# Weight sums of a seven-product gate: from VectorE additions to accumulating transfers

## The chip, the cores and the metric

The kernel runs on one core of a Trainium2 chip. The metric is the device time of one execution in microseconds; the median of several executions is compared. TensorE multiplies, VectorE (DVE) and ScalarE (ACT) work elementwise, GpSimd (POOL) and SyncE (SP) are used here only to issue transfers.

## The reference

The program is a stack of four layers on a 512 x 1024 input in fp32: two layers of a first kind (spatial gating, a state-space mixer, differential attention, three gates, a feed-forward part), then two of a second kind. The change touches the gates of the first kind. Of each such layer, cut to what matters:

```python
proj = h @ w_in[layer]                       # h: 512 x 1024
g = sigmoid(gates).reshape(b, s, 3, 1024)    # gates: the last 3072 columns of proj
merged = (g[:, :, 0] * (y_a @ w_branch_a[layer])
          + g[:, :, 1] * (y_b @ w_branch_b[layer])
          + g[:, :, 2] * (y_c @ w_branch_c[layer]))
x = x + merged @ w_out[layer]
```

## The kernel before, in words

Every fp32 matmul is made of three: a weight tile `wr` that a transfer has brought is split by ScalarE into a rounded part `wh` (a cast) and by VectorE into the rest `wl = wr - wh`; the activations are split in the same way, and `mm3` (L512) adds high x high, high x low and low x high in PSUM. A weight tile holds 2 x 128 rows and 512 columns, 512 KB. There are four `wr` buffers and three each of `wh` and `wl`. PSUM has four `pm` banks and four `px` banks.

**Order of the work.** No engine call runs directly. The class `Order` records each one (`record`, L185) with a cost, a priority and its dependences; `schedule` (L240) lays all of them out in time by that model, and `issue` (L380) emits them in this order and pins the order on each engine's queue. A call made inside `hurry` or with a `bonus` gets a priority far ahead of its place. A transfer is modelled as its bytes over 360 per ns on one shared line (L204), plus 740 ns after SyncE's issue and 2240 ns after GpSimd's (`LANDED`, L132). `after=op` makes a call wait for `op` in this model.

**The gates.** `layer1` (L1062) makes the first gate with plain matmuls and the other two (columns of `w_in`, 1024 wide) with `tm7` (L583), a scheme of Strassen's kind: the 1024 x 1024 weights are cut into quarters b11, b12, b21, b22 of 512 x 512, and seven products of a half of the tokens with a quarter or a sum of quarters, instead of eight, give the gate. The combinations of the activations are made once in `combos` (L555). A product is 24 matmuls of 512 columns into two banks and needs two `wr` tiles ("halves", of 256 rows). Before, each quarter is loaded once. VectorE makes the sums: `q` = b11 + b12 in four heap slots of 512 columns, later `q` += b22, then `q` += b21 (four operations each), and b12 += b22 in place (two operations of 1024 columns). The products run in the order b11, q, q, b12, b22, b21, q; the first `q` product goes into `px`. Their results are combined in the gate's tiles `sg` and go through a tanh (`fin`). This runs in four stages: third and second gate of each layer of the first kind. Between them lie the products of `branch`.

**The parameters.** `load_params1` (L805) brings the packs `pn`, `pa` and `pb` at a layer's start, for the first layer on SyncE's queue, for the second on GpSimd's. `pa` has 3180 columns, 1590 KB. At once it derives `nlam`, `nega`, `slg2` and `wt` from `lam`, `alog`, `slg` and `ws` in it. In the first layer the constants `cst` (592 KB) follow on SyncE's queue; `norm` (L692) needs the ones in them.

## Time and profile before

| | us |
|---|---|
| median of 3 runs | 2515.24 (2515.04 to 2518.61) |
| the profiled execution | 2517.48 |
| its span, first to last instruction | 2515.6 |
| TensorE busy | 2496.1 |
| VectorE busy | 1742.5 |
| ScalarE busy | 1215.3 |
| GpSimd busy | 52.7 |
| transfers of SyncE's queue | 241.03 MB |
| transfers of GpSimd's queue | 20.33 MB |

The span is that of one profiled execution; the time of the same execution is 1.9 us longer. "Busy" of TensorE counts overlapping matmuls once, so it does not tell at what pace they follow each other; the pace is read from a stretch of the chain and the number of matmuls in it. Nearly all instructions carry one line (L385, where `issue` emits them), so the rows are told apart by the names of the tiles: out<-in. The chain is the work that ended last, followed back from the last instruction.

### The profile page before, as it was taken

What the parts mean: (1) busy time and instruction counts of PE and PEld (TensorE: products, weight loads), DVE (VectorE), ACT (ScalarE), POOL (GpSimd) and SP (SyncE); (2) the same over time, 40 slices, a digit from 0 to 9 for tenths busy, and PEclk for the clock granted to TensorE, in tenths of its full rate; (3) what the DMA queues carried; (4) which work ended last, traced back from release to release, by engine and by line L of the source; (5) the groups of instructions that cost most, each with busy time, mean ns of one, the idle gap of its engine ahead of it and who ended that gap; (6) DMA issues with size and microseconds to landing.
All of it is one profiled execution on the core that took longest, in us unless ns stands there. A gap on an engine that the chain in (4) does not pass through costs nothing.

```text
span 2515.6 us, 33045 instructions
## 1 busy us (share of the span) xinstructions
PE 2496.1 (99%) x12158; PEld 2111.6 (84%) x12158; DVE 1742.5 (69%) x3497; ACT 1215.3 (48%) x2210; POOL 52.7 (2%) x103
## 2 busy tenths in 40 slices
PE   8999999999999999999999999999999999999999
PEld 7888888888888888898888888888898888988887
DVE  7679878657566346598878486663369987679783
ACT  5494734434444234757544254442247564356552
POOL 0000000000000000101000000000000000000000
PEclk9999999999999999999999999999999999999999
DMA  7444343343333444434343343333433123432222
GB/s 219 100 120 105 70 110 101 109 150 102 100 95 116 133 111 78 152 66 101 85 107 102 101 143 101 96 97 117 137 109 97 54 68 95 142 105 68 68 76 84
DMA packets 160642, 263.48 MB, mean 105 GB/s; under 512 B 11504, under 2 KB 71296, under 8 KB 160224
## 3 DMA queue, kind: packets, MB, share of 16 engines
q1 hardware_dynamic: 152864, 241.03, 34.0%
q0 software_dynamic: 7616, 20.33, 2.9%
q8 instruction: 96, 1.57, 0.3%
q14 instruction: 66, 0.54, 0.1%
HBM read 241.33 MB, written 14.75 MB: 102 GB/s over the span
## 4 chain that ended last, share of the span: by engine, by line
PE 88%; DVE 7%; DMA 2%; ACT 1%; issue 1%; SPq 0%; DVEq 0%; ACTq 0%
PE pm L385 68%; PE px L385 20%; DVE wl L385 2%; DMA wr<-in_w_in_dram 2%; DVE sg L385 1%; DMA pa<-in_pa_dram 1%; ACT p L385 1%; DVE q L385 0%; DVE p L385 0%; DVE sptl L385 0%; DMA cst<-in_cst_dram 0%; ACT wh L385 0%; DVE so L385 0%; SPq L385 0%; DVE gs L385 0%
## 5 line engine op out<-in xcount | busy, mean ns | idle before, releaser
L385 DVE TENSOR_TENSOR wl<-wr,wh 128x1024 fp32r<-128x1024 f32 (+3 forms) x413 | 488.9, 1185 | 598.9 <-ACT wh L385 593.9
L385 ACT CAST wh<-wr 128x1024 fp32r<-128x1024 f32 (+3 forms) x413 | 421.6, 1022 | 828.3 <-PE pm L385 658.3
L385 PE MATMUL pm<-wh,hh 128*128 128x512 f32 (+2 forms) x608 | 229.5, 377 | 0.0
L385 PE MATMUL pm<-wl,hh 128*128 128x512 f32 (+2 forms) x608 | 227.3, 374 | 0.0
L385 PE MATMUL pm<-wh,hl 128*128 128x512 f32 (+2 forms) x608 | 225.8, 374 | 0.0
L385 PE MATMUL pm<-hh,wh 128*128 128x512 f32 x512 | 199.8, 390 | 0.0
L385 PE MATMUL pm<-hh,wl 128*128 128x512 f32 x512 | 199.5, 390 | 0.0
L385 PE MATMUL pm<-hl,wh 128*128 128x512 f32 x512 | 199.2, 389 | 0.0
L385 PE MATMUL pm<-gl,wh 128*128 128x512 f32 x384 | 154.1, 401 | 0.0
L385 PE MATMUL pm<-gh,wh 128*128 128x512 f32 x384 | 153.3, 399 | 0.0
L385 PE MATMUL pm<-gh,wl 128*128 128x512 f32 x384 | 152.5, 397 | 0.0
L385 PE MATMUL pm<-wh,gh 128*128 128x512 f32 (+2 forms) x384 | 143.6, 375 | 0.9 <-ACT wh L385 0.9
L385 PE MATMUL pm<-wl,gh 128*128 128x512 f32 (+2 forms) x384 | 143.4, 374 | 0.0
L385 PE MATMUL pm<-wh,gl 128*128 128x512 f32 (+2 forms) x384 | 142.6, 372 | 0.0
L385 PE MATMUL pm<-acth,wh 128*128 128x512 f32 x352 | 136.9, 389 | 0.0
L385 PE MATMUL pm<-actl,wh 128*128 128x512 f32 x352 | 136.9, 389 | 0.0
L385 PE MATMUL pm<-acth,wl 128*128 128x512 f32 x352 | 136.9, 389 | 0.0
L385 PEld LDWEIGHTS pm<-wh,hh 128*128 128x128 f32 x608 | 114.3, 188 | 15.7 <-issue 3.3
L385 PEld LDWEIGHTS pm<-wl,hh 128*128 128x128 f32 x608 | 114.4, 188 | 14.3 <-issue 1.9
L385 PEld LDWEIGHTS pm<-wh,hl 128*128 128x128 f32 x608 | 114.3, 188 | 13.8 <-issue 1.4
L385 PE MATMUL px<-hl,wh 128*128 128x512 f32 x320 | 124.5, 389 | 0.0
L385 PE MATMUL px<-hh,wl 128*128 128x512 f32 x320 | 124.5, 389 | 0.0
(479 smaller groups left out, 5669.1 us busy)
## 6 DMA issues: line engine op xcount, KB each, us to landing
wr<-in_w_in_dram SPq DMA_DIRECT2D x151, 512.0 KB, 3.8
wr<-in_ffn_w_up_dram SPq DMA_DIRECT2D x176, 256.0 KB, 3.1
wr<-in_ffn_w_down_dram SPq DMA_DIRECT2D x44, 512.0 KB, 3.5
wr<-in_w_out_dram SPq DMA_DIRECT2D x40, 512.0 KB, 3.6
wr<-in_w_in_dram SPq DMA_DIRECT2D x40, 384.0 KB, 3.5
xr<-xd SPq DMA_DIRECT2D x48, 256.0 KB, 4.9
xd<-xr SPq DMA_DIRECT2D x40, 256.0 KB, 3.2
m<-ad POOLq DMA_DIRECT2D x32, 256.0 KB, 7.3
```

Of the source, the lines that this page charges most:

```text
L385: ins = f(*args, **kw).ins
```

## The change

`tm7` no longer adds quarters on VectorE. `q` and `b2` are now pairs of `wr` tiles: SyncE loads a quarter into them, and transfers on GpSimd's queue with `accum_op=ALU.add` add another quarter from HBM to what lies there. b11 is loaded twice, b22 fetched three times (once plainly), b21 and b12 as the sums need them. The order of products is b11, b21, q = b11 + b12, b2 = b12 + b22, q += b22, b22, q += b21, and all go into `pm`. Loading with four `wr` buffers becomes loading with five (NWR, also in `wload`). To a layer's `pa` pack the columns of `ws`, `lam`, `slg` and `alog` (912 of 3180) no longer belong; two packs `pl` (400 columns) and `pw` (512) bring them on GpSimd's queue into heap slots, after the first matmuls of the layer (`late_params1`, called in `layer1`), and what was derived from them is derived there. The planner's model counts an accumulating transfer at half the rate.

```diff
--- before.py
+++ after.py
@@ -24,6 +24,7 @@
 KD = D // P
 EPS = 1e-6
 NSLOT = 68
+NWR = 5
 NPM = 4
 
 GM = 512
@@ -79,10 +80,10 @@
     "pn": [("ang", "attn_norm_g", columns, 8)],
     "pa": [("cw", "ssm_conv_w", columns, 48), ("cb", "ssm_conv_b", columns, 12),
            ("bs", "gm_b_s", rows, 512), ("vg", "gm_v_norm_g", rows, 512), ("dtb", "ssm_dt_bias", rows, 16),
-           ("alog", "ssm_a_log", rows, 16), ("dsk", "ssm_d", rows, 16), ("sng", "ssm_norm_g", rows, 1024),
-           ("qg", "da_q_norm_g", rows, 64), ("kg", "da_k_norm_g", rows, 64), ("slg", "da_subln_g", rows, 128),
-           ("lam", "da_lambda", rows, 256),
-           ("ws", "gm_w_s", lambda v: v.transpose(2, 0, 1).reshape(P, -1), 512)],
+           ("dsk", "ssm_d", rows, 16), ("sng", "ssm_norm_g", rows, 1024),
+           ("qg", "da_q_norm_g", rows, 64), ("kg", "da_k_norm_g", rows, 64)],
+    "pw": [("ws", "gm_w_s", lambda v: v.transpose(2, 0, 1).reshape(P, -1), 512)],
+    "pl": [("lam", "da_lambda", rows, 256), ("slg", "da_subln_g", rows, 128), ("alog", "ssm_a_log", rows, 16)],
     "pb": [("fng", "ffn_norm_g", columns, 8), ("fcw", "ffn_conv_w", columns, 132), ("fcb", "ffn_conv_b", columns, 44)],
     "pc": [("ng", "norm_g_2", columns, 8), ("qag", "mla_q_a_norm_2", columns, 2), ("kvg", "mla_kv_a_norm_2", columns, 1),
            ("cw2", "conv_w_2", lambda v: v.reshape(3, 4, P).transpose(2, 0, 1).reshape(P, -1), 12),
@@ -201,7 +202,7 @@
             n = 4.0
             for d in outs[0].shape:
                 n *= d
-            op.dma = n / 360.0
+            op.dma = n / (180.0 if "accum_op" in kw else 360.0)
         op.succ, op.bufs = [], set()
         deps = {after: 0} if after is not None else {}
         for ap, wr in [(a, False) for a in ins] + [(a, True) for a in outs]:
@@ -442,10 +443,11 @@
     def pmix(self):
         return self.tile(self.px, [P, T], F32, "px", "px", 8 - NPM)
 
-    def pack(self, key, l, eng=None):
+    def pack(self, key, l, eng=None, temp=False, op=None):
         items = PACK[key]
-        t = self.param(key, sum(i[3] for i in items))
-        (eng or self.nc.gpsimd).dma_start(out=t, in_=self.a[key][l])
+        n = sum(i[3] for i in items)
+        t = self.slot(key, [P, n]) if temp else self.param(key, n)
+        (eng or self.nc.gpsimd).dma_start(out=t, in_=self.a[key][l], after=op)
         q, o = {}, 0
         for nm, _, _, n in items:
             q[nm] = t[:, o:o + n]
@@ -491,7 +493,7 @@
         nc = self.nc
         n = sum(c[1] for c in cols)
         keep, nc.bonus = nc.bonus, bonus
-        wr = self.tile(self.wp, [P, nk, n], F32, "wr", "wr", 4)
+        wr = self.tile(self.wp, [P, nk, n], F32, "wr", "wr", NWR)
         off = 0
         for c0, cn in cols:
             nc.sync.dma_start(out=wr[:, :, off:off + cn],
@@ -582,8 +584,11 @@
 
     def tm7(self, w, c0, parts, c, fin):
 
+
         nc = self.nc
         v = nc.vector
+        rows = lambda kh, u: slice((kh * 4 + u * 2) * P, (kh * 4 + u * 2 + 2) * P)
+        cols = lambda ch: slice(c0 + ch * 512, c0 + (ch + 1) * 512)
 
         def hurry(f, *args):
             keep, nc.bonus = nc.bonus, 1000000
@@ -594,30 +599,28 @@
         def load(kh, ch):
             out = []
             for u in range(2):
-                wr = self.tile(self.wp, [P, 2, 512], F32, "wr", "wr", 4)
-                r0 = (kh * 4 + u * 2) * P
-                nc.sync.dma_start(out=wr, in_=w[r0:r0 + 2 * P, c0 + ch * 512:c0 + (ch + 1) * 512].rearrange("(k p) f -> p k f", p=P))
+                wr = self.tile(self.wp, [P, 2, 512], F32, "wr", "wr", NWR)
+                nc.sync.dma_start(out=wr, in_=w[rows(kh, u), cols(ch)].rearrange("(k p) f -> p k f", p=P))
                 out.append(wr)
             return out
 
+        def add(d, kh, ch):
+            for u in range(2):
+                nc.gpsimd.dma_start(out=d[u], in_=w[rows(kh, u), cols(ch)].rearrange("(k p) f -> p k f", p=P), accum_op=ALU.add)
+            return d
+
         def split_w(src):
             out = []
-            for u in range(2):
+            for wr in src:
                 wh = self.tile(self.wp, [P, 2, 512], F32R, "wh", "wh", 3)
                 wl = self.tile(self.wp, [P, 2, 512], F32R, "wl", "wl", 3)
-                for o, i, h in ([(wl, src[u], wh)] if len(src) == 2 else
-                                [(wl[:, kk, :], src[2 * u + kk], wh[:, kk, :]) for kk in range(2)]):
-                    nc.scalar.copy(out=h, in_=i)
-                    v.tensor_sub(out=o, in0=i, in1=h.bitcast(F32))
+                nc.scalar.copy(out=wh, in_=wr)
+                v.tensor_sub(out=wl, in0=wr, in1=wh.bitcast(F32))
                 out.append((wh, wl))
             return out
 
-        def add(q, b):
-            for k in range(4):
-                v.tensor_add(out=q[k], in0=q[k], in1=b[k // 2][:, k % 2, :])
-
-        def product(ws, part, mixed=False):
-            ps = [self.pmix() if mixed else self.pmain() for _ in range(2)]
+        def product(ws, part):
+            ps = [self.pmain() for _ in range(2)]
             for t in range(2):
                 for k in range(4):
                     wh, wl = ws[k // 2]
@@ -631,51 +634,46 @@
         def room(t0, half):
             for t in range(2):
                 c[t0 + t][half] = self.slot("sg")
-        b11 = hurry(load, 0, 0)
-        p1 = product(hurry(split_w, b11), parts["A11"])
+        p1 = product(hurry(split_w, hurry(load, 0, 0)), parts["A11"])
+        room(2, 0)
+        each(lambda t: nc.scalar.copy(out=c[2 + t][0], in_=p1[t]))
+        q = hurry(load, 0, 0)
+        hurry(add, q, 0, 1)
+        p2 = product(hurry(split_w, hurry(load, 1, 0)), parts["A12"])
         room(0, 0)
-        each(lambda t: nc.scalar.copy(out=c[t][0], in_=p1[t]))
-        b12 = hurry(load, 0, 1)
-        q = [self.slot("q") for _ in range(4)]
-
-        def first_sum():
-            for k in range(4):
-                v.tensor_add(out=q[k], in0=b11[k // 2][:, k % 2, :], in1=b12[k // 2][:, k % 2, :])
-        hurry(first_sum)
-        p5 = product(hurry(split_w, q), parts["D"], True)
-        b22 = hurry(load, 1, 1)
-        hurry(add, q, b22)
+
+        def upper(t):
+            v.tensor_add(out=c[t][0], in0=p2[t], in1=c[2 + t][0])
+            fin(t, 0, c[t][0])
+        each(upper)
+        b2 = hurry(load, 0, 1)
+        hurry(add, b2, 1, 1)
+        p5 = product(hurry(split_w, q), parts["D"])
+        room(2, 1)
+        each(lambda t: nc.scalar.copy(out=c[2 + t][1], in_=p5[t]))
+        hurry(add, q, 1, 1)
+        p7 = product(hurry(split_w, b2), parts["R7"])
+        room(0, 1)
+
+        def seventh(t):
+            v.tensor_add(out=c[2 + t][0], in0=c[2 + t][0], in1=p7[t])
+            v.tensor_add(out=c[t][1], in0=c[2 + t][1], in1=p7[t])
+        each(seventh)
         p6 = product(hurry(split_w, q), parts["R6"])
-        room(2, 0)
-        room(0, 1)
-
-        def both(t):
-            v.tensor_add(out=c[2 + t][0], in0=p6[t], in1=c[t][0])
-            v.tensor_sub(out=c[t][1], in0=p5[t], in1=c[2 + t][0])
-        each(both)
-
-        def second_sum():
-            for u in range(2):
-                v.tensor_add(out=b12[u], in0=b12[u], in1=b22[u])
-        hurry(second_sum)
-        p7 = product(hurry(split_w, b12), parts["R7"])
-        room(2, 1)
-
-        def lower(t):
-            v.tensor_sub(out=c[2 + t][1], in0=c[t][1], in1=p7[t])
+
+        def sixth(t):
+            v.tensor_add(out=c[2 + t][0], in0=c[2 + t][0], in1=p6[t])
+            for u in (2 + t, t):
+                v.tensor_sub(out=c[u][1], in0=c[u][1], in1=c[2 + t][0])
             fin(2 + t, 1, c[2 + t][1])
-            v.tensor_add(out=c[2 + t][0], in0=c[2 + t][0], in1=p7[t])
-        each(lower)
-        p3 = product(hurry(split_w, b22), parts["R3"])
+        each(sixth)
+        hurry(add, q, 1, 0)
+        p3 = product(hurry(split_w, hurry(load, 1, 1)), parts["R3"])
 
         def plus(t, half, ps):
             v.tensor_add(out=c[t][half], in0=c[t][half], in1=ps)
             fin(t, half, c[t][half])
         each(lambda t: plus(t, 1, p3[t]))
-        b21 = hurry(load, 1, 0)
-        p2 = product(hurry(split_w, b21), parts["A12"])
-        each(lambda t: plus(t, 0, p2[t]))
-        hurry(add, q, b21)
         p4 = product(hurry(split_w, q), parts["A22"])
         each(lambda t: plus(2 + t, 0, p4[t]))
 
@@ -807,6 +805,12 @@
         q = self.pn if l == 0 else self.pack("pn", l)
         q.update(self.pack("pa", l, nc.sync if l == 0 else None))
         q.update(self.pack("pb", l, nc.sync if l == 0 else None))
+        return q
+
+    def late_params1(self, q, l, op):
+        nc = self.nc
+        for key in ("pl", "pw"):
+            q.update(self.pack(key, l, None, True, op))
         lam_init = 0.8 - 0.6 * math.exp(-0.3 * l)
         d2 = self.small("d2", 2)
         tmp = self.slot("lamt", [P, 64])
@@ -826,7 +830,6 @@
         q["wt"] = self.param("wt", 512)
         nc.vector.tensor_tensor(out=q["wt"].rearrange("p (g t) -> p g t", g=4), in0=q["ws"].rearrange("p (g t) -> p g t", g=4),
                                 in1=self.tri.unsqueeze(1).to_broadcast([P, 4, P]), op=ALU.mult)
-        return q
 
     def gm_mix(self, q, u, v):
         nc = self.nc
@@ -1064,6 +1067,7 @@
         q = self.load_params1(l)
         w = a["w_in"][l]
         hg, r, rb, scaled = self.norm(x, q["ang"])
+        marks = []
         u, v = [None] * NT, [None] * NT
 
         def ev_gelu(dst):
@@ -1075,9 +1079,10 @@
             u[j] = self.slot("gel")
             nc.vector.tensor_mul(out=u[j], in0=ps, in1=rb)
             nc.scalar.activation(out=u[j], in_=u[j], func=AF.Gelu_apprx_tanh)
-        self.tm(w, C_V, 512, hg, ev_gelu(v))
+        self.tm(w, C_V, 512, hg, ev_gelu(v), marks.append)
         self.fm(w, [(C_U, 512)], hg, ev_u)
         h = scaled()
+        self.late_params1(q, l, marks.pop())
         u = self.gm_mix(q, u, v)
         xbc = [None] * 12
 
...
```

## Rows read from the trace of the kernel before

**Rows 1.** The page: busy us (share of the span) xinstructions.

```profile
PE 2496.1 (99%) x12158; PEld 2111.6 (84%) x12158; DVE 1742.5 (69%) x3497; ACT 1215.3 (48%) x2210; POOL 52.7 (2%) x103
```

**Rows 2.** The page: the chain that ended last, by engine.

```profile
PE 88%; DVE 7%; DMA 2%; ACT 1%; issue 1%; SPq 0%; DVEq 0%; ACTq 0%
```

**Rows 3.** Windows of the four stages: us, busy PE PEld DVE ACT POOL, clock, transfer share, GB/s.

```profile
366.95:406.20 39.25, 38.36 (x169) 31.41 (x168) 32.19 (x46) 20.16 (x29) 0.00 (x0) 1.00 0.38 104
429.98:468.56 38.58, 38.36 (x169) 31.41 (x168) 33.92 (x50) 20.23 (x29) 0.00 (x0) 1.00 0.39 108
1274.84:1313.89 39.05, 38.38 (x169) 31.40 (x168) 32.12 (x46) 20.13 (x29) 0.00 (x0) 1.00 0.39 105
1337.67:1376.25 38.58, 38.57 (x171) 31.56 (x170) 33.87 (x49) 20.09 (x29) 0.00 (x0) 1.00 0.38 109
```

**Rows 4.** Chain in order of time, second product on: start us, us, what.

```profile
368.22 4.90 DMA wr<-in_w_in_dram
...
374.37 0.61 DVE wl L385
...
375.03 4.13 PE px L385 x17
379.16 27.20 PE pm L385 x120
```

**Rows 5.** What TensorE waited for, whole span: us in total, times, longest.

```profile
PE px L385 <- DMA xin<-in_x_dram: 4.5, 1, 4.5
PE px L385 <- DMA cst<-in_cst_dram: 2.4, 1, 2.4
...
PE px L385 <- DVE wl L385: 1.8, 3, 0.9
PE px L385 <- DVE mgl L385: 1.6, 2, 0.8
```

**Rows 6.** Chain in order of time, the start: start us, us, what.

```profile
8.68 13.57 DMA pa<-in_pa_dram
...
22.27 8.64 DMA cst<-in_cst_dram
```

**Rows 7.** Groups of the first stage: shapes xcount | busy us, mean ns | idle before.

```profile
L385 DVE TENSOR_TENSOR wl<-wr,wh 128x1024 fp32r<-128x1024 f32 x9 | 10.9, 1221 | 3.3 <-ACT wh L385 3.3
...
L385 ACT CAST wh<-wr 128x1024 fp32r<-128x1024 f32 x8 | 8.4, 1052 | 4.9 <-PE pm L385 3.3 <-issue 1.4 <-PE px L385 0.2
L385 DVE TENSOR_TENSOR wl<-q,wh 128x512 fp32r<-128x512 f32 x12 | 7.9, 687 | 1.9 <-ACT wh L385 1.9
L385 ACT CAST wh<-q 128x512 fp32r<-128x512 f32 x12 | 6.9, 619 | 10.5 <-PE pm L385 6.0 <-PE px L385 3.7 <-DVE q L385 0.8
...
L385 DVE TENSOR_TENSOR sg<-sg,pm 128x512 f32<-128x512 f32 x9 | 5.9, 681 | 0.1
L385 DVE TENSOR_TENSOR q<-q,wr 128x512 f32<-128x512 f32 x8 | 5.2, 685 | 0.0
```

**Rows 8.** Transfers by line, whole span: queue, count, KB, median us to landing.

```profile
wr<-in_w_in_dram SPq DMA_DIRECT2D x151, 512.0 KB, 3.8
...
m<-ad POOLq DMA_DIRECT2D x32, 256.0 KB, 7.3
...
pa<-in_pa_dram POOLq DMA_DIRECT2D x1, 1590.0 KB, 6.7
...
mw<-in_mla_w_kvb_dram POOLq DMA_DIRECT2D x4, 256.0 KB, 3.3
```

**Rows 9.** Timeline: start us, us, engine, operation; the fourth product of the first stage.

```profile
383.28 1.05 ACT L385 CAST wh<-wr 128x1024 fp32r<-128x1024 f32 x1 [2.97 <-PE pm L385]
384.37 1.23 DVE L385 TENSOR_TENSOR wl<-wr,wh 128x1024 fp32r<-128x1024 f32 x1 [1.03 <-ACT wh L385]
```

**Rows 10.** Window of the start, columns as in rows 3.

```profile
22.00:31.00 9.00, 6.65 (x30) 5.18 (x28) 6.59 (x20) 4.07 (x9) 0.00 (x0) 1.00 1.04 365
```

**Rows 11.** Window in which GpSimd issues the `m` transfers, columns as in rows 3.

```profile
121.00:135.00 14.00, 14.00 (x65) 11.51 (x64) 10.70 (x14) 11.50 (x18) 8.19 (x16) 1.00 0.74 257
```

## What is expected of the change

> **What bounds the kernel now.** I read the engine totals first: TensorE is busy for 2496.1 of the span's 2515.6 us, VectorE for 1742.5 [rows 1]. The chain that ended last says the same by what it is made of: 88% of it is TensorE, 7% VectorE, 2% transfers [rows 2]. So a change that leaves the number of matmuls alone, as this one does, can only give back time in which TensorE stands still, and the next views look for that in the two places that the diff touches.
>
> The first is the four stages of seven products (two gates in each of two layers) [rows 3]. A product is 24 matmuls; the chain carries 120 of them in 27.20 us [rows 4], so 226.7 ns each and 5.44 us a product; seven take 38.09 us. The four stages last 39.25, 38.58, 39.05 and 38.58 us, together 155.46 against 4 x 38.09 = 152.35: **3.1 us are lost in all four.** Most of it is one place per stage: the second half of the weights of the second product is late (the chain runs through a 4.90 us load, VectorE's sum behind it and a `wl`, and only then TensorE again [rows 4]; all waits of TensorE for `wl` are 1.8 us in three places [rows 5]). VectorE is busy for 32 to 34 us of a stage, the transfer engines at a share of 0.38 to 0.39, and the clock is granted in full [rows 3].
>
> The second is the start. The chain goes through the 13.57 us of `pa` and then the 8.64 us of `cst` [rows 6], which SyncE issues in the moment `pa` has landed; TensorE waits 2.4 us for `cst` [rows 5].
>
> **The change part by part.**
> *The sums leave VectorE.* Per stage it drops 12 sums of 512 columns at 0.685 us and two of 1024, at 1.221 like a `wl`: 10.7 us; with 12 splits of 512 (0.687) replaced by 6 of 1024 (1.221) another 0.9; the new order adds two evictions at 0.68 [rows 7]. About 10 us less in a stage, 41 in all. ScalarE trades 12 casts of 0.619 for 6 of 1.052 (1.1 us less) and gets two more copies of 512 columns, at most 0.62 each [rows 7]. I cost all of it at nothing, since TensorE's 38.1 us cover both engines; VectorE's relief counts only by removing the late `wl`. The fifth product's result moves from the `px` banks into the four `pm` banks, so each pair must be emptied within the next product, 5.44 us; the longest eviction (sixth product) frees its second bank after four operations at 0.69, 2.8 us. Nothing again.
>
> *The transfers that take the sums' place.* A stage goes from 8 loads of 512 KB to 10, plus 8 accumulating transfers of 512 KB on GpSimd's queue, which is empty in these stages (busy 0.00 [rows 3]), so they pass nobody there. No row shows an accumulating transfer. Plain ones from the same queue: 256 KB of `mw` 3.3 us, 1590 KB of `pa` 6.7 [rows 8]; on the line between them 512 KB would take 3.9 us, 1.3 of it data. An accumulate must also read its target. *Lower bound: 3.9 us (the reading is free). Taken: 5.3 us (the 1.3 us of data twice). Upper bound: 10.6 us, twice that;* the broadcasts `m`, at 7.3 us for 256 KB in bursts [rows 8], show that this queue can be so slow when its transfers pile up. I take 5.3 because the HBM rows of known size are the nearest, and the target lies in SBUF.
>
> What waits for them is ScalarE's cast of a half, and behind that cast in its queue stand evictions and the next casts; TensorE follows. How much time is there? From the fourth product of the first stage, which starts at 379.16 + 5.44 = 384.6 [rows 4]: its second half is cast from 383.28, and VectorE has read it by 385.60 [rows 9]. So a second half is read from 1.3 us before to 1.0 us after its product starts. A first half must be picked up 2.6 us before (cast 1.05, subtraction 1.22, hops).
> - `q` is read for the third product, then accumulated, then read for the fifth, two products later: 10.88 - 1.0 - 1.3 = **8.6 us**. The same from the fifth to the seventh.
> - `b2` (for the fourth product, due at 16.32 - 1.3 = 15.0 us after the first product starts): its second half takes the buffer that the second product's first half leaves at about 2.7 (cast and subtraction begin when the split buffers of the product before come free, at 0); a load of 4.9 us [rows 4] brings it to 7.6. Left: **7.4 us**. First half: free at 1.0, loaded at 5.9, due at 16.32 - 2.6 = 13.7: 7.8 us.
>
> The need: 5.3 alone. For `b2`'s second half add 1.0 behind its twin on the same queue and 1.4 behind one load (0.524 MB at the 365 GB/s of the full queues [rows 10]): 7.7, so 0.3 late. For `q` 5.3 + 1.4 = 6.7: 1.9 to spare. Four stages: **+1.2 us**. The engines' room agrees: 18 x 0.524 MB, and 8 x 0.524 read back, is 13.6 MB, at 365 GB/s 37.3 us of the stage's 38.1. Nearly all of it: there is no reserve.
>
> *Late sums on VectorE gone:* with the data in time the 3.1 us of today go: **-3.1**.
>
> *Parameters.* `pa` loses 912 of its 3180 columns, 456 KB, and at 365 GB/s lands 1.3 us sooner; `cst` starts that much sooner. But the 456 KB come back as `pl` and `pw` on GpSimd's queue after the first matmuls, so perhaps still ahead of `cst` in the same saturated transfer engines (share 1.04 [rows 10]). Between -1.3 and 0; I take **-0.6**. Their few small operations (`wt`, of 512 columns like the sums at 0.685, is the longest) move from the start into VectorE's time under the first products, which lie before their first use.
>
> *Five weight buffers.* A load can be issued one step of 5.44 us sooner. Loads land in 3.8 us at the median [rows 8] and TensorE's only waits for transfers are at the start [rows 5], so nothing by itself; without it `q` could not stay resident. The planner reorders the whole program; I price that at 0, ±1.
>
> Sum: -3.1 + 1.2 - 0.6 = **-2.5 us**. The profiled execution took 2517.48 us, 1.9 beyond its span, and is 2.24 above the median of the three runs; the sum applies to either. From the median: 2515.24 - 2.5 = **2512.7 us**. About 0.2%, 5.0 us, is what a measurement of this kernel can tell from no change.
>
> **The rivals.**
> *A. The accumulates are slower than their slack (slower).* One mechanism: read-modify-write on the transfer engines in the four stages. It decides above 5.0 us alone for `b2` and 7.2 for `q`. At 7.3 us alone: `b2` late by 7.3 + 2.4 - 7.4 = 2.3, the seventh product by 0.1 (the fifth's wait is swallowed by the fourth's): 2.4 x 4 = +9.6, less 3.7: 2521. At 10.6: 5.6 + 3.4 = 9.0 x 4 = +36, less 3.7: 2547.5. For it: 37.3 of 38.1 us of transfer time on my own count, and `m`. Against: plain transfers from that queue keep their pace. Chance 0.33.
> *B. GpSimd can't write its descriptors while VectorE works (slower).* VectorE is busy in 85% of such a stage. In the stretch where GpSimd issues most, 121 to 135 us, VectorE is busy 10.70 of 14 us and sixteen issues of GpSimd still take 8.19 us, 0.51 each [rows 11], so I give it little. Its price, if an issue had to sit out two subtractions of 1.22 us: a transfer of 5.3 + 2.4 = 7.7 alone, so (2.7 + 0.5) x 4 = +12.8, less 3.7: 2524. Chance 0.05.
> The Trainium skill, page "SBUF — State Buffer", section "SBUF: two separate sides" (the "DVE blocks DMA" trap), has this rule: a transfer from GpSimd's queue that takes about 620 ns alone takes about 3100 beside a VectorE copy in a two-port mode. By that page, as an estimate, a transfer would lose 2.5 us and the kernel would come to 2525. The trace speaks against it here: the stage's VectorE work is two-input subtractions at 1221 ns for 1024 columns [rows 7], and the issues of `m` beside VectorE are not longer.
> *C. More comes back than I count (faster).* All 2.4 us at the start, all 3.1 in the stages, and the 1.6 us that TensorE waits for `mgl` behind the second gate [rows 5], as VectorE arrives there less loaded: -7.1, 2508.1. Against: that wait hangs on the last merge, not on sums. Chance 0.15.
>
> **How the numbers follow.** Forecast 0.47 (from -4.4, accumulates at 3.9 us and `cst` fully sooner, to +5). A 0.33, B 0.05, C 0.15. Faster by over 0.2%: C, 0.15. Within: 0.47. Slower: A and B, 0.38. The forecast's own range, with the ±1 of the order, is 2510 to 2520; for 8 in 10 it must reach into A: 2508 to 2543.
>
> **What would show it.** Right: transfers into `wr` from GpSimd's queue landing in 5 to 6.5 us; VectorE near 23 us busy in a stage; stages of 38.1 to 38.5 us; no `q` sums. A: TensorE or ScalarE's `wh` waiting for transfers into `wr` in the fourth, fifth and seventh products, stages of 40 us and more, transfer share near 1. B: long gaps between GpSimd's issues. The start: `cst` issued near 21 us, and its wait gone or not. I am wrong in the mechanism if stages keep a late `wl` with transfers in time.

## The result: 20 us slower, all of it in the four stages

The changed kernel takes 2534.98 us (median of 4 runs, 2533.92 to 2538.16) against 2515.33 us (4 runs) of the kernel before on the same chip: ratio 1.0076, 95% interval 1.0064 to 1.0088. That is the side of rival A. The profiled execution took 2538.16 us, 1.8 beyond its span, and is 20.7 us above the profiled one of before.

The page of the kernel after, busy us by engine, and the chain that ended last by engine:

```profile
PE 2503.6 (99%) x12158; PEld 2114.1 (83%) x12158; DVE 1707.9 (67%) x3425; ACT 1219.3 (48%) x2197; POOL 93.1 (4%) x139
...
PE 87%; DVE 6%; DMA 4%; ACT 2%; issue 1%; SPq 0%; POOL 0%; ACTq 0%; POOLq 0%; DVEq 0%
```

VectorE is busy 35 us less than in [rows 1], of the 41 that the sums were costed at, and the end did not care. The matmuls are the same 12158, yet TensorE is busy 7.5 us longer, and the share of transfers in the chain has doubled [rows 2]. To place the loss I took, in each trace, the last matmul of the branch ahead of a stage and the last of the branch behind it. Every whole kernel of this study has these points, and the differences to the kernel before are (us, from one profiled execution of each; a stage's column includes the branch behind it):

| kernel | start, to the first branch | stage 1 | stage 2 | stage 3 | stage 4 | span |
|---|---|---|---|---|---|---|
| after | +0.13 | +4.36 | +7.60 | +4.77 | +3.77 | +20.73 |
| e1_plain | -0.01 | +0.43 | +1.23 | +1.11 | +3.53 | +6.69 |
| e2_half | +2.95 | +6.01 | +5.56 | +3.30 | +3.88 | +22.20 |
| e3_vec | +2.54 | +0.26 | +0.10 | +1.19 | +0.23 | +4.67 |
| e4_old_half | -0.16 | -0.19 | +0.49 | +0.15 | +0.65 | +0.71 |
| f1_plain_pack | +0.12 | -1.21 | -0.51 | -0.95 | -0.33 | -2.71 |
| f2_acc_pack | +1.15 | -1.20 | -0.55 | -0.99 | +0.16 | -0.79 |
| f3_old_pack | -1.22 | -1.23 | -0.50 | -0.97 | -0.33 | -4.52 |
| f4_late_sp | +0.27 | +0.05 | +0.03 | +0.68 | +0.21 | +1.16 |
| g2_old_all | -5.61 | -1.21 | -0.51 | -1.04 | -0.34 | -9.14 |
| g3_acc_all | -1.42 | -1.19 | -0.50 | -0.94 | -0.33 | -4.21 |
| h2_pad | -2.13 | -1.19 | -0.54 | -1.00 | -0.33 | -5.34 |
| h3_2k | +1.82 | -1.15 | +0.14 | +0.43 | +0.15 | +1.61 |
| h4_late_all | -3.72 | -1.20 | -0.51 | -0.99 | -0.35 | -6.95 |
| i2_old_pad | -3.82 | -1.19 | -0.50 | -0.96 | -0.33 | -6.93 |
| i3_acc_pad_sp | -5.32 | -1.04 | -0.50 | +0.38 | +0.27 | -6.11 |

The changed kernel loses 20.5 of its 20.7 us in the stages. Windows of 42 us from the first matmul of each stage on (columns as in [rows 3]):

```profile
367.07:409.10 42.03, 38.97 (x170) 31.20 (x169) 24.65 (x28) 20.57 (x27) 7.09 (x6) 0.96 0.90 169
434.46:476.50 42.04, 37.34 (x154) 29.70 (x153) 23.45 (x29) 18.10 (x22) 7.12 (x6) 0.92 0.85 156
1286.88:1329.10 42.22, 38.78 (x170) 31.17 (x169) 24.88 (x29) 20.70 (x27) 7.08 (x6) 0.96 0.88 167
1354.48:1396.50 42.02, 38.78 (x176) 31.24 (x175) 27.25 (x34) 21.01 (x27) 7.12 (x6) 1.00 0.90 174
```

VectorE fell to 23 to 27 us (the forecast had near 23); the transfer engines' share went from 0.38 to 0.9 [rows 3]; and in three stages the granted clock is below 1. What TensorE waited for in the whole span (answers to [rows 5]), the timeline of ScalarE in the fourth and fifth products of the first stage (to [rows 9]), and the transfers into `wr` by GpSimd's queue, on the page and from 369 to 400 us, with what either queue took of the engines there (packets, MB, share):

```profile
PE pm L386 <- ACT wh L386: 12.1, 9, 3.3
PE px L386 <- DMA xin<-in_x_dram: 6.5, 2, 4.4
PE pm L386 <- DVE wl L386: 3.0, 4, 0.8
```

```profile
384.74 1.04 ACT L386 CAST wh<-wr 128x1024 fp32r<-128x1024 f32 x1 [3.29 <-DMA wr<-in_w_in_dram]
...
395.89 1.04 ACT L386 CAST wh<-wr 128x1024 fp32r<-128x1024 f32 x1 [3.72 <-DMA wr<-in_w_in_dram]
```

```profile
wr<-in_w_in_dram POOLq DMA_DIRECT2D x32, 512.0 KB, 8.6
...
L386 POOL DMA_DIRECT2D wr<-in_w_in_dram x6: 1172/1178/1654, 369.8 to 398.5; - x6
...
DMA to landing us min/median/max: 5.8/8.7/16.4
...
q0 software_dynamic: 1358, 2.62, 59.8%
q1 hardware_dynamic: 1360, 2.62, 38.0%
```

The quickest accumulate lands in 5.8 us; a piled-up one needs up to 16.4. The second half of `b2` is cast at 384.74 when its transfer lands, and the second half of `q` for the fifth product at 395.89. The seventh product is in time. Behind these stalls comes a second loss, the clock (windows of the pile-up, and of what lies behind the fourth product's stall in the first stage and around the fifth product's in the second and third):

```profile
377.00:384.00 7.00, 7.00 (x32) 5.79 (x32) 2.96 (x3) 3.16 (x4) 2.20 (x2) 1.00 1.08 164
384.00:391.00 7.00, 5.32 (x18) 3.69 (x17) 3.73 (x4) 2.47 (x3) 0.00 (x0) 0.81 1.05 151
...
384.50:392.50 8.00, 6.32 (x20) 4.45 (x19) 4.03 (x5) 3.52 (x4) 0.00 (x0) 0.79 1.05 155
460.80:470.50 9.70, 6.42 (x17) 4.74 (x16) 3.17 (x4) 2.09 (x2) 1.59 (x2) 0.65 0.87 194
1313.00:1320.50 7.50, 5.50 (x18) 4.02 (x17) 3.20 (x4) 2.09 (x2) 1.62 (x2) 0.77 0.93 188
```

In the first stage matmuls start 427 ns apart instead of 227 from 388 to 392 us, which is 1.2 instead of 2.4 GHz, after TensorE had stood still twice for about 1.1 us. In the second and third stage the same pace follows one stall of 3.4 and of 2.2 us in the fifth product; in the fourth stage a stall of 2.2 us in that place leaves the clock at 1.00. The last three windows lose 8.0 x 0.21 + 9.7 x 0.35 + 7.5 x 0.23 = 6.8 us of clock. TensorE stood still in a part of them; counted by matmuls, 28 spacings of about 427 ns instead of 227 lose 5.6. The waits for `wh` and `wl` grew from 0.9 and 1.8 us to 12.1 and 3.0, 12.4 more. Together 18.0 to 19.2 of the 20.5 us.

The first line of this fence has the engines full (1.08) while they move 164 GB/s, where the forecast had taken 365. But that rate alone does not make a stall, since half of what moves around there is accumulates. The kernel h2_pad below, which waits for no transfer in the stages, has such a window too:

```profile
375.00:382.00 7.00, 7.00 (x32) 5.82 (x31) 3.86 (x4) 4.63 (x7) 2.26 (x2) 1.00 1.00 165
```

What is particular to the changed kernel has to be found with the adding taken out.

### The profile page after: what moved, and what is told of

It is laid out like the page before. It is cut to its first block, busy times and chain, and to the rows that moved or that the text cites. A ratio compares the mean times of both kernels' runs of the same rounds, so it can differ in the third digit from the quotient of the medians.

```text
span 2536.4 us, 33129 instructions
## 1 busy us (share of the span) xinstructions
PE 2503.6 (99%) x12158; PEld 2114.1 (83%) x12158; DVE 1707.9 (67%) x3425; ACT 1219.3 (48%) x2197; POOL 93.1 (4%) x139
## 4 chain that ended last, share of the span: by engine, by line
PE 87%; DVE 6%; DMA 4%; ACT 2%; issue 1%; SPq 0%; POOL 0%; ACTq 0%; POOLq 0%; DVEq 0%
PE pm L386 68%; PE px L386 19%; DMA wr<-in_w_in_dram 3%; DVE wl L386 1%; ACT wh L386 1%; DVE sg L386 1%; DMA pa<-in_pa_dram 1%; ACT p L386 1%; DVE p L386 0%; DVE sptl L386 0%; DVE q L386 0%; DMA cst<-in_cst_dram 0%; DVE so L386 0%; DVE gs L386 0%; DVE k L386 0%
## 5 line engine op out<-in xcount | busy, mean ns | idle before, releaser
L386 DVE TENSOR_TENSOR wl<-wr,wh 128x1024 fp32r<-128x1024 f32 (+4 forms) x437 | 517.5, 1187 | 670.1 <-ACT wh L386 664.9
L386 ACT CAST wh<-wr 128x1024 fp32r<-128x1024 f32 (+4 forms) x437 | 446.4, 1023 | 884.0 <-PE pm L386 609.9
```

Of the source, the lines that this page charges most:

```text
L386: ins = f(*args, **kw).ins
```

## The experiments

**e1_plain: the same order on every engine, nothing is added.**

```
-  accum_op=ALU.add)
+  )        # planner's price for the transfer kept
```

> The changed kernel in the same order on every engine, but the 32 transfers on GpSimd's queue overwrite instead of adding (the sums of quarters are left out). Theory 1 (reading and writing back the target doubles the packets' time, and the transfer engines are full in the stages): with plain packets the four stages return to 38.1 to 38.5 us each, the transfers land in 4 to 5 us instead of 8.6, and the kernel takes 2513 to 2518 us. Theory 2 (GpSimd's queue itself: its issues of 1.18 us in order, each behind the one before): the same bytes come as late as before, stages of 42 us, 2530 to 2536 us.

Measured: 2524.88 us, ratio 1.0035 (1.0022 to 1.0048). That lies between the two expectations. Two thirds of the stages' loss go with the adding, 6.3 us stay. The queues' shares of the engines in 32 us of the first stage, the landings of GpSimd's six transfers in it, now plain, and the window of the pile-up:

```profile
q0 software_dynamic: 864, 3.15, 45.7%
q1 hardware_dynamic: 1652, 3.17, 45.6%
...
DMA to landing us min/median/max: 5.9/8.3/10.8
...
384.00:391.00 7.00, 5.94 (x26) 4.37 (x25) 4.50 (x5) 4.00 (x5) 0.00 (x0) 1.00 0.99 160
```

So plain transfers pile up too, and this is the line to hold on to: the engines are full (0.99) at 160 GB/s with nothing to add. 3.17 MB of SyncE's (three loads of `w_in`, three of `w_branch_c`) take 0.456 x 32 = 14.6 us of all engines, 4.6 us a MB, where 365 GB/s would be 2.7. Something makes the reading itself slow.

**e2_half, e4_old_half: the first weight half for both token tiles, then the second** (in the changed kernel and in the one before), so that a late second half has six matmuls, 1.4 us, more.

```
-  for t in range(2):
-      for k in range(4):
+  for t, k in [(t, 2 * u + j) for u in range(2) for t in range(2) for j in range(2)]:
```

> The changed kernel, but a product runs the first weight half for both token tiles, then the second half for both: the second half is due 12 matmuls after the product's start instead of 6, so 1.36 us later. Theory 1a (each accumulate misses its due time by a fixed 1.5 to 3.5 us): two waits per stage shrink by 1.36 us each, 4 x 2.7 = 11 us, and the stretches at half clock behind them shorten or go: 2519 to 2525 us. Theory 1b (the transfer engines are full, so everything only shifts): less than 4 us come back, 2530 to 2536 us.

> The kernel before with the same exchange of loops in a product: the late wl of the second product in each stage (1.8 us in three places, 3.1 us lost in all four stages) is due 1.36 us later. If it is late by about 1 us: the loss goes, 2512 to 2513 us. If the load behind it only sets a later time for everything: 2515 us, no change.

Measured: e2 2537.61 us, ratio 1.0083 (1.0066 to 1.0099); e4 2516.69, 1.0003 (0.9993 to 1.0012). Later due times do not help after the change. That is what full engines would make of it, where everything only shifts; other reasons were not tried. Before the change they take the late `wl` away, and the time comes back in a new place, the stage's end (TensorE's waits in that window):

```profile
PE pm L385 <- ACT ych L385: 1.0, 1, 1.0
```

**e3_vec: the new order, five buffers and late parameters, but the sums on VectorE** (`b21` loaded twice).

```
-  nc.gpsimd.dma_start(out=d[u], in_=w[...], accum_op=ALU.add)
+  v.tensor_add(out=q[k], in0=q[k], in1=b[k // 2][:, k % 2, :])
```

> The changed kernel's order of products, five weight buffers and later parameters, but the sums on VectorE again (b21 is loaded a second time, no accumulating transfer). If the loss is all the accumulates': stages of 38.1 to 38.8 us, 2511 to 2516 us. If the new order of products with all results in the pm banks costs something itself: stages of 39.5 us and more, 2520 us and more.

Measured: 2521.89 us, ratio 1.0020 (1.0010 to 1.0029). By time that is the second case, by place it is not: the stages lose 1.8 us in all, the start 2.5. Order and buffers do not make the 20.5 us; the loss needs the eight more transfers of a stage on GpSimd's queue.

**f1_plain_pack, f2_acc_pack, f3_old_pack: the gates' columns of `w_in` in contiguous blocks,** in e1_plain, in the changed kernel and in the kernel before.

```
+  g = data["w_in"][:, :, C_GATE:].reshape(2, 4, 2, P, 6, 512)
+  data["w_gate"] = np.ascontiguousarray(g.transpose(0, 4, 1, 3, 2, 5))
-  in_=w[rows(kh, u), cols(ch)].rearrange("(k p) f -> p k f", p=P)
+  in_=w[c0 + ch, kh * 2 + u]
```

> The changed kernel with the adding taken out of its GpSimd transfers (they overwrite, so q and b2 hold a quarter in place of a sum; e1_plain), and in addition the gate columns of w_in laid out by the host as contiguous blocks, 4 KB for each partition, so that a row of 2 KB no longer lies 32,832 bytes from the next. Order on every engine as in the changed kernel. Theory 1 (what fills the transfer engines in the stages is the reading of w_in in short pieces far apart, by two queues at once): the four stages lose their 6.2 us over the kernel before; a GpSimd transfer lands in 4 to 5.5 us where e1_plain had 8.2 to 10.8, no wait for wr in the fourth and fifth products, 2516 to 2520. Theory 2 (it is the amount of data on two queues, wherever it lies): as e1_plain, 2523 to 2527.

> The changed kernel as it is, accumulates included, with the gate columns of w_in as contiguous blocks. Theory 1 (short pieces far apart are the limit, adding costs little by itself): accumulates land in 5 to 7 us, the stalls of the fourth and fifth products and the half clock behind them go, 2515 to 2521. Theory 2 (reading the target and writing it back in 2 KB packets is the limit): stays within 3 us of the changed kernel, 2532 to 2538, landings still 13 to 16 us in the pile-up. Between: 2522 to 2531, if each carries a part.

> The kernel before with the same contiguous blocks for the gates of its four stages, nothing else. Its transfer engines are at a share of 0.38 in a stage, so theory 1 gives faster landings (3.8 us to about 3) and, where the late second half of the second product's weights hangs on a load of 4.9 us, up to 0.6 us in a stage: 2513 to 2516. Theory 2: no change within 1 us.

Measured: 2516.14 us, ratio 0.9996 (0.9987 to 1.0005); 2515.88, 0.9995 (0.9986 to 1.0004); 2512.89, 0.9983 (0.9974 to 0.9992). With the accumulates all in place the 20.5 us are gone and the stages give 2.6 of the 3.1 us that the forecast had counted on. The same view as for e1_plain, of f2_acc_pack, and then GpSimd's queue and its landings in f1_plain_pack:

```profile
q0 software_dynamic: 864, 3.15, 57.1%
q1 hardware_dynamic: 1223, 3.11, 26.1%
...
DMA to landing us min/median/max: 5.4/5.7/8.1
...
q0 software_dynamic: 864, 3.15, 29.0%
...
DMA to landing us min/median/max: 3.5/3.6/4.7
```

SyncE's 3.11 MB now cost 0.261 x 32 = 8.4 us, 2.7 a MB. GpSimd's plain transfers cost 2.9 a MB where e1_plain's cost 4.6, and land in 3.6 us instead of 8.3; its accumulates cost 5.8, twice as much as the plain ones. And f3_old_pack shows that the kernel before had the same illness in a mild form: its late `wl` in the stages hung on a slow load, and goes without any change of order.

**f4_late_sp: the kernel before with the parameters' part alone, `pl` and `pw` on SyncE's queue behind `cst`.**

```
+  q.update(self.pack(key, l, nc.sync, True, op))      # key in ("pl", "pw")
```

> The kernel before with the parameters' part of the change alone (pa split into pa, pl and pw), but pl and pw issued on SyncE's queue behind cst instead of GpSimd's. Theory S (the changed kernel's start loses by pl and pw being issued at 1.9 and 2.4 us, ahead of the tiles of x, so that x lands 2 us and cst 1 us later): x lands as in the kernel before, cst is issued about 1.3 us sooner than its 22.27 us and lands near 29.6, TensorE's wait for cst shrinks from 2.4 to about 1.2 us: 2513.5 to 2515.5. Rival (the order of what is cast and split first sets the start, not the transfers): no change within 1 us, or the half clock behind the wait stays as it is.

Measured: 2519.07 us, ratio 1.0012 (1.0003 to 1.0020). The chain at the start (to [rows 6]) and the windows behind the wait for `cst`:

```profile
8.72 12.40 DMA pa<-in_pa_dram
...
21.14 8.75 DMA cst<-in_cst_dram
```

```profile
31.00:34.00 3.00, 3.00 (x11) 2.40 (x11) 2.47 (x15) 0.49 (x1) 0.00 (x0) 0.71 0.90 275
34.00:37.00 3.00, 3.00 (x11) 2.36 (x11) 2.23 (x8) 1.48 (x2) 0.00 (x0) 0.73 1.07 386
```

`cst` is issued 1.1 us sooner and lands 1.0 us sooner. But TensorE still waits 2.5 us for it and then runs at the lower clock for some 3 us, as in the kernel before. The forecast's mechanism is there, but it pays nothing: the run is 0.1% slower than the kernel before, and theory S is missed.

**g1_rates, h1_cold, i1_lone: loads by themselves,** streams of 512 KB, streams over rows not read before, and one load at a time, quiet and beside busy engines.

```
+  for n in range(N):
+      (nc.gpsimd if on_pool else nc.sync).dma_start(out=bufs[n], in_=src(n), **kw)
+  settle(N)
```

> No stage at all: the kernel only loads pieces of 512 KB (128 x 2 x 512) into eight buffers, in phases divided by a VectorE read of all of them, and writes what is in four of them as its output. Phases of eight: SyncE's queue alone from w_in (2 KB pieces, rows 32,832 bytes apart), ffn_w_up (22,528), w_in_2 (17,024), w_out (4,096), and w_out as whole rows of 4 KB; then GpSimd's queue alone and both queues in turn from w_in and w_out; each plain and accumulating, and a single transfer of each. Theory 1 (short pieces 32.8 KB apart are what is slow, whoever asks): in the kernel before, two loads of w_in at the start land 3.95 us apart (133 GB/s) and tiles of x, rows 4 KB apart, 0.64 us apart for half as much (about 400 GB/s). So eight of w_in take 24 to 32 us on either queue and on both together, eight of w_out 10 to 13 us; a single accumulate lands in 5.5 to 6.5 us from w_in and at most 1 us sooner from w_out; eight accumulates over both kinds of rows differ as the plain ones do. Rival (two queues at once are what is slow): SyncE's queue alone takes 10 to 13 us for eight from w_in, and only the phases on both queues go down to 130 to 180 GB/s.

> Loads only, as g1_rates, but of pieces that no phase before has read, since g1_rates read the same quarters of w_in again and again and found 331 GB/s on SyncE's queue where the kernel before gets 133. Each phase is eight loads of 512 KB: eight column blocks of the same 256 rows, then the same again; eight pieces each from other rows than the one before, then again; then on both queues in turn, plain and with accumulates on GpSimd's, each twice, from w_in and from a copy whose rows are padded to 34,816 bytes. Theory D (rows 32,832 bytes apart are slow where a load comes to rows it has not just read): first passes over new rows take 3 to 4 us for each 512 KB, second passes and passes along the same rows 1.3 to 1.6, and the padded copy 1.3 to 1.6 throughout. Rival W (it is the kernel's other work, engines and writes, that slows these reads): all passes 1.3 to 1.7 us for plain loads, as in g1_rates, w_in and padded copy alike.

> Loads only, but one at a time: eight pieces of 512 KB of the third gate on SyncE's queue, each issued when the one before has been read by ScalarE, then four pairs of the second gate, one piece on either queue at once. From w_in (rows 32,832 bytes apart), from a copy padded to 34,816, and from w_out (4,096). First quiet (layer 0), then (layer 1) with the same loads while TensorE runs matmuls, ScalarE casts and VectorE subtractions of a split. Theory D (the distance of the rows is enough): quiet loads from w_in land in 3.6 to 4.5 us and pairs in 5.5 to 9, the other two sources in 3.2 to 3.5 and 4 to 5; the same with work beside them. Theory W (it takes the engines' work beside the transfers): quiet, all three sources within 0.3 us of each other; with work, w_in alone is slower by 0.5 us or more. Neither: no difference between the sources in either half; then what makes w_in slow in the kernel stays open beyond the fact that the distance of its rows decides it there.

Measured: neither theory's numbers. In g1_rates SyncE's queue alone, from `w_in` and then from `w_out` (columns: us, VectorE, GpSimd, clock, share, GB/s):

```profile
5.00:17.00 12.00, 5.08 (x13) 0.00 (x0) 1.00 0.90 341
...
30.00:39.00 9.00, 0.92 (x6) 0.00 (x0) 1.00 1.05 387
```

Eight accumulates from `w_in` landed 3.3 us apart, 160 GB/s, with SyncE's next loads beside them, and from `w_out` no sooner. In h1_cold the phases ran into each other; on SyncE's queue alone its first pass over new rows took 1.3 to 3.0 us for a load, and two pieces that were slow in it (2.3 and 3.0 us) were slow again in the second pass (2.6 and 3.3), so it is not that they were new. In windows of 12 to 15 us the engines moved 262 to 390 GB/s. In i1_lone GpSimd's queue ran ahead of its pairs, through the quiet half, so neither tells anything. In the half with the engines busy SyncE's single loads landed like this (four loads each from `w_in`, the padded copy and `w_out`):

```profile
DMA to landing us min/median/max: 3.7/4.3/4.8
...
DMA to landing us min/median/max: 3.6/3.6/3.8
...
DMA to landing us min/median/max: 3.7/3.8/4.3
```

Over all twelve loads of each the medians are 4.2, 3.6 and 3.8 us. Of those from `w_in` six, the first column block of each two, took 4.5 to 4.8 us, the other six 3.7 to 3.9. So a single load shows the distance, by half a microsecond at the median. But none of the three runs shows plain loads at the 160 GB/s of e1_plain's stage. The rows' distance is not slow in every stream, and what else it needs was not found.

**h2_pad, h3_2k: in the changed kernel, rows 34,816 bytes apart instead of 32,832 (nothing else), or pieces of 2 KB placed one behind the other.**

```
+  data["w_in"] = np.pad(data["w_in"], ((0, 0), (0, 0), (0, 496)))
```

> The changed kernel with w_in padded by the host with 496 columns of zeros: rows 34,816 bytes apart instead of 32,832, pieces of 2 KB as far apart as before, the same order on all engines. Theory D (the distance of 32,832 bytes itself): as f2_acc_pack, 2514 to 2519. Rival Q (pieces of 2 KB, or rows far apart at whatever distance, are slow): 2530 to 2538, as the changed kernel.

> f2_acc_pack with the blocks laid out row after row: pieces of 2 KB as in the changed kernel, but 2 KB apart. Theory D: 2514.5 to 2519, the smaller pieces costing at most an issue of 1.18 in place of 0.86 us on GpSimd. Rival Q in its first half (the size of the piece): 2525 or more.

Measured: h2_pad **2512.20 us**, ratio 0.9983 (0.9973 to 0.9992); h3_2k 2518.08, 1.0005 (0.9996 to 1.0014). One line on the host turns the changed kernel from 0.8% slower into 0.2% faster; the time is even below theory D's range. The stages of h2_pad, then the queues in 32 us of the first one and GpSimd's landings:

```profile
364.81:403.31 38.50, 38.50 (x179) 31.91 (x178) 26.53 (x32) 21.14 (x27) 7.09 (x6) 1.00 0.81 190
426.66:465.20 38.54, 38.54 (x179) 31.95 (x178) 27.76 (x35) 21.14 (x27) 7.12 (x6) 1.00 0.81 192
1270.85:1309.40 38.55, 38.55 (x179) 31.97 (x178) 26.59 (x32) 21.14 (x27) 7.08 (x6) 1.00 0.81 192
1332.68:1371.20 38.52, 38.52 (x178) 31.90 (x177) 27.73 (x35) 21.14 (x27) 7.12 (x6) 1.00 0.81 190
```

```profile
q0 software_dynamic: 1632, 3.15, 59.6%
q1 hardware_dynamic: 1580, 3.07, 26.8%
...
DMA to landing us min/median/max: 5.8/6.1/9.6
```

TensorE is busy in every microsecond of these windows. The pieces are as short and as far apart as in the changed kernel, so it is neither the 2 KB nor the distance in general, but this distance. Where a piece begins is no better than before either: the gates start at column 5136, 20,544 bytes into rows of 34,816, which puts every piece 64 bytes behind a multiple of 512 as counted from the tensor's start. Other distances were not tried in the kernel. h3_2k's stages give 0.4 us where f2_acc_pack's give 2.6, so close pieces of 2 KB are not quite as good as pieces of 4 KB, but that is a tenth of the loss in question.

**g2_old_all, g3_acc_all, h4_late_all: all blocks of `w_in` contiguous,** in the kernel before, in the changed one, and in f4_late_sp. **i2_old_pad, i3_acc_pad_sp: `w_in` padded,** in the kernel before, and in the changed one with `pl` and `pw` on SyncE's queue.

```
+  for n, cs in BLOCKS.items():      # the column blocks, by width
+      g = [w[:, :, c:c + n].reshape(2, 4, 2, P, n).transpose(0, 1, 3, 2, 4) for c in cs]
+      data[f"w_in_{n}"] = np.ascontiguousarray(np.stack(g, axis=1))
```

> The kernel before with every column block of w_in that is loaded as one piece laid out contiguously by the host (the gates as in f3_old_pack, and the blocks of the other loads too). Theory 1: at the start two loads of w_in land 1.3 us apart in place of 3.95, pa lands some 5 us sooner, cst near 26 us, TensorE's wait for cst (2.4 us) and the half clock behind it (some 1.7 us) go; the stages give the 3 us they gave in f3_old_pack: 2508.5 to 2511. Rival (the start hangs on the order of the work, not on the transfers): 2512 to 2514, as f3_old_pack.

> The changed kernel with the same layout for all of w_in. Theory 1: the stages stay at 38.2 to 38.6 us as in f2_acc_pack, and the start, where pl and pw still go ahead of x, gains at least 2 us: 2510 to 2514, level with or up to 2 us above g2_old_all. Rival: no gain on f2_acc_pack, 2514.5 to 2517.

> g2_old_all (the kernel before with all of w_in in blocks) with the parameters split as in the change, pl and pw on SyncE's queue behind cst, as in f4_late_sp. Theory S (pl and pw cost the changed kernel's start only because GpSimd's queue sends them ahead of x): pa lands 1.2 us sooner than the 17.67 us of g2_old_all, cst as well, but TensorE no longer waits for cst there, so no change within 1 us of g2_old_all's 2509.05. Rival (the split itself costs the start 2 to 4 us, through the order of what is cast first): 2511 to 2513.

> The kernel before with w_in padded to 34,816 bytes a row, nothing else. Theory D: the late second half of the second product's weights goes (3 us over the four stages, as in f3_old_pack), the two loads of w_in at the start land about 1.3 us apart, cst lands 4 us sooner and is no longer waited for: 2508 to 2511, level with g2_old_all. Rival (only pieces of 4 KB help the order of before): 2514 to 2517.

> The changed kernel with w_in padded and with pl and pw on SyncE's queue, behind cst: the change with both of the causes found so far taken away. Stages as in h2_pad (all four 38.1 to 38.3 us), start as in i2_old_pad: 2508.5 to 2511, no better than i2_old_pad, since the stages have nothing left to give. Rival (the changed kernel's order of casts still costs the start): 2511.5 to 2513.5, as h2_pad.

Measured: **g2 2509.05 us, ratio 0.9972 (0.9961 to 0.9982)**; g3 2514.54, 0.9994 (0.9985 to 1.0002); h4 2510.42, 0.9973 (0.9963 to 0.9983); **i2 2510.64, 0.9970 (0.9959 to 0.9981)**; i3 2511.66, 0.9978 (0.9969 to 0.9987). The kernel before with the new layout beats both kernels. At the start of g2 two loads of `w_in` land 1.27 us apart (at 12.44 and 13.71 us), in the kernel before 3.95 us (at 14.40 and 18.35); the wait for `cst` and the lower clock behind it are gone (windows of g2, the wait was at 28 to 31 us):

```profile
25.00:28.00 3.00, 3.00 (x19) 2.61 (x18) 3.00 (x6) 0.30 (x1) 0.00 (x0) 1.00 1.05 401
28.00:31.00 3.00, 3.00 (x15) 2.44 (x15) 2.55 (x16) 0.52 (x1) 0.00 (x0) 1.00 1.04 418
```

g3 against g2 and i3 against i2 say what the change itself is worth on good rows: at best nothing in the stages, since the old order reaches their floor as well (-3.0 against -3.1 us in the table), and a loss at the start as long as GpSimd's queue carries `pl` and `pw`; g3 fell to its rival. With them on SyncE's queue i3 and i2 lie within each other's intervals. But i3's time, too, is its rival's (2511.5 to 2513.5), and not by the start, where it gives 5.3 us: in the stages it gives 0.9 where i2 gives 3.0, with two waits for `wl`, 1.1 us, that h2_pad does not have.

## Why the prediction was wrong

*What bounds the kernel* held: TensorE alone, 3.1 us to be had in the stages. h2_pad and g2_old_all got 3.1 of them.

*The accumulate's own price* held nearly: taken 5.3 us, bounds 3.9 and 10.6; the quickest land in 5.4 (f2_acc_pack) and 5.8 us. "The 1.3 us of data twice" is close as well: 6.1 us a MB against 2.8 for plain loads in h2_pad (0.596 x 32 / 3.15 and 0.268 x 32 / 3.07).

**The step that failed is the one on the company:** "add 1.0 behind its twin on the same queue and 1.4 behind one load (0.524 MB at the 365 GB/s of the full queues [rows 10])", and with it "37.3 us of the stage's 38.1". The 365 GB/s came from a window in which the transfers are of all kinds. In the changed stages a MB cost 4.5 us of the engines on SyncE's queue and 7.1 on GpSimd's (e1_plain: 4.6 for plain loads). By these rates a stage's transfers are 5.24 x 4.5 + 4.19 x 7.1 = 53 us of work, by h2_pad's 5.24 x 2.8 + 4.19 x 6.1 = 40, by the forecast's 37.3. The sum itself decides nothing, as h2_pad's 40 are more than 38.1 and it stands still nowhere: a part of the work is done ahead (the first two accumulates go out at 347.48 and 356.28 us, the stage's first matmul starts at 367.07). What the slow rows change is when the piled-up transfers land. `b2`'s second half took 9.0 us and `q`'s second half for the fifth product 16.4, where the step had 7.7 and 6.7; in h2_pad the same two took 6.0 and 9.6. So the step was short for `q` even on good rows: it put `q` behind one load, while three accumulates go out within 4 us on the one queue. The trace of before had the row. It is the window between the two landings of `w_in` at the start, 3.95 us apart (133 GB/s for the second load); here it stands for the kernel before, and then for i2_old_pad, whose rows alone are different (columns as in [rows 3]):

```profile
14.40:18.35 3.95, 3.95 (x23) 3.35 (x22) 3.95 (x6) 3.18 (x6) 0.00 (x0) 1.00 1.00 264
```

```profile
14.40:18.35 3.95, 3.95 (x24) 3.37 (x23) 3.60 (x5) 3.83 (x7) 0.00 (x0) 1.00 0.96 391
```

Full engines at 264 GB/s, with part of `pa` among it, some eight microseconds ahead of the window that the forecast took its rate from.

The cause is the distance of `w_in`'s rows: f2_acc_pack and h2_pad show it from two sides. The Trainium skill has a row on such distances, page "DMA: Bandwidth & Descriptors", section "Latency and other measured facts": copies between HBM tensors slow down where rows lie a large power of two apart, 512 KiB and more in its measurement, a few KiB of padding restore the rate and 192 bytes do not. The row does not reach down to 32 KiB plus 64 bytes; what agrees with it here is the remedy, h2_pad's 1,984 bytes of padding (2534.98 to 2512.20 us). The mechanism that the page supposes is not shown by any run here.

*Late sums on VectorE gone, -3.1*: the amount was right, the reason half right. The late `wl` hung on a load of 4.9 us [rows 4] as much as on the sums; f3_old_pack removes it with the sums on VectorE.

*Parameters, -0.6 (between -1.3 and 0)*: nothing came of it. The runs with this start and the old rows there (the changed kernel, e1, e2, e3, f1, f2, h3) lie from 0.0 to +3.0 us in the table. The step said that they are issued "after the first matmuls", on the word of the planner's order. But no wait stands behind that order on GpSimd's queue, and both go out ahead of six of the eight tiles of `x` (timeline of GpSimd after):

```profile
1.92 0.54 POOL L386 DMA_DIRECT2D pl<-in_pl_dram  x1
2.44 0.54 POOL L386 DMA_DIRECT2D pw<-in_pw_dram  x1
```

The wait for `x` grew from 4.5 to 6.5 us and `cst` went out at 24.76 instead of 22.27. In the profiled execution the clock stayed up behind the shorter wait for `cst` (1.3 us), which evens it out (+0.13); e3_vec, with the same parameters, waited 2.7 us for VectorE there and lost 2.54.

*Evictions, order, five buffers at 0*: held within 2 us (e3_vec's stages, +1.8; h2_pad's reach the floor). *The seventh product's slack*: held.

*The rivals.* A was right in sign and place, the fourth and fifth products, and its range of 2521 to 2547.5 holds the result. Its mechanism is half of what happened: adding takes twice the engines' time, and two thirds of the loss go with it (e1_plain). But on other rows the same accumulates stall next to nothing (f2_acc_pack, h2_pad), and the accumulate alone is fast enough: by A's own formula 5.8 us would have made (5.8 + 2.4 - 7.4) x 4 = +3.2, less 3.7, no change. A also priced the stalls without the clock that falls behind them, 5.6 to 6.8 us. B did not happen: GpSimd issues its six accumulates in 1.17 to 1.65 us each while VectorE is busy 24.65 of 42 us, and what delays them is the landing. C's 2508.1 is about what g2_old_all reached, for the most part by C's first two terms, but by the layout and not by the change.

## What to carry to other kernels

Before a rate goes into a sum, take it from loads of the very tensor, between two landings of the same queue, and not from a window in which other tensors' rows raise the mean. Where rows lie just beside a power of two apart (here 32 KiB plus 64 bytes), try a padded copy or contiguous blocks first: here it was worth more than either kernel's order of work. An order that only a planner knows delays nothing on an idle queue; a transfer that must come later needs a wait or a place behind others.

## What was not expected of the hardware

Plain transfers, most of them from rows 32,832 bytes apart, filled the transfer engines at 160 GB/s in a stage of e1_plain, and with rows 34,816 bytes apart the changed kernel does not wait for a transfer in the stages. That streams of loads alone do not show it (341 GB/s in g1_rates), and single loads only by half a microsecond (i1_lone), stays open. An accumulating transfer takes about twice the engine time of a plain one of the same size (5.8 against 2.9 us a MB), and GpSimd needs 1.18 us to issue one of 256 rows of 2 KB, 0.86 for 128 rows of 4 KB (f2_acc_pack). And TensorE's stalls drew about half as much again in clock: 5.6 to 6.8 us behind 12.4.
